# First G loaded in four pieces, its transposes moved forward, seven U blocks multiplied as split pairs, and 110 instead of 108 blocks of U ahead of the loop

## The chip, the cores and the metric

The kernel runs on one core of one Trainium2 chip. The metric is the device time of one execution in microseconds (us). The median of three runs of the kernel before the change is 1488.86 us (1487.65 to 1489.21). The engines are TensorE (PE in the profile, with its weight loads as PEld), VectorE (DVE), ScalarE (ACT), GpSimd (POOL) and SyncE (SP). ACT and SP issue ordinary DMAs, POOL issues the indirect ones that gather table rows.

## The reference

The program is one encoder layer on 512 tokens of width 1024: two kinds of attention, a LayerNorm, and then a product-key expert layer (PEER) with a gate, followed by a second LayerNorm. The change touches only the expert layer:

```
idx = e1 * 128 + e2                        # 8 heads x 16 picks = 128 experts of 16384 per token
g   = softmax(cv)                          # their weights
hpre = einsum('td,ted->te', x, U[idx])     # U: 16384 x 1024
act  = g * gelu(hpre)
out  = einsum('te,ted->td', act, V[idx])   # V: 16384 x 1024
h    = LN2(alpha*h + out + sigmoid(h @ W_g + b_g) * (p @ W_ple))
```

## The kernel before, in words

**Two ways through the experts.** The first 128 tokens (chunk 0) are served by gathers: POOL fetches one row of U, later of V, per token and expert, and DVE does the dot product or the weighted sum. The other 384 tokens are served densely. For each of the 128 blocks of 128 experts there is a matrix G (experts of the block x tokens, mostly zeros) with the router's weights. For 256 of the tokens the kernel computes gelu(U_block . h) on TensorE, multiplies it into G on DVE, and multiplies the product with the V block on TensorE, which adds up the output in PSUM. The 128 tokens in between (chunk 1, "own" in the code: `N_S = 128`) get their U values by gathers, folded into G beforehand, and only their V side is dense.

**Products before the loop.** `gate_and_leads` is a generator of TensorE work: one step is one matmul, and a block of U is eight of them (`lead_block`, line 1291) in plain float32. `LEAD` blocks of U are done so, ahead of the loop. Their gelu results (`ge`) go to a DRAM tensor for the first `SPILL = 96` blocks, and stay on chip for the others: `KEPT_K` of them in tiles that the gate no longer needs, the rest in eight `ge` tiles. U is loaded into three `raw` tiles and one `raw_u` tile by SP, in turn.

**What sets the order.** The order is written out by hand. The router (`route`), the construction of G (`build_g`, 16 steps per chunk of 128 tokens: one-hot matrices `oh_i` and `oh_j` on DVE and ACT, sixteen small products on TensorE at line 1115, results `g_st` copied out by ACT at line 1128) and the row gathers of the own chunk (`own_rows`) and of chunk 0 (`beside`) are generators too. `run_pe(amount)` puts TensorE steps worth `amount` us behind them into the queue, so the constants `WAIT`, `LAG`, `PACE`, `OWN_G` and so on decide how much U work stands between two steps of the G work. The G of a chunk begins with three transposes (line 1090) of its expert numbers and weights. Chunks 2 and 3 come first; the own chunk's G is built last, because it needs the gathered values. Finished G goes out to DRAM in quarters (`send`, line 1073, by ACT).

**The first G.** The loop reads G in groups of eight blocks (`GB = 8`), of twelve token groups each, ten of them from DRAM. The group of the first eight blocks (`first_g`) is loaded before the own chunk is built, in one DMA of eight token groups (line 1447), after all quarters have been sent.

**The loop.** It goes over 128 blocks (`order`): DVE multiplies `ge` into G (line 1598), ACT and DVE cut V and G into a high part in the reduced type float32r and a rest (`split`, line 110), and TensorE does 18 matmuls of 512 columns (line 1551). From the ninth block on (`KEPT = 8`) it also does the blocks of U that are left (`expert_in`: split pair, 24 matmuls of 256 columns at lines 129 to 131), one per iteration, until U is done. Gathers for chunk 0 are spread over the iterations in proportion to a weight (1 with a block of U, `LATE = 0.57` without). `load_g` loads the next group of G in four parts; in which iterations is set by one condition:

```
if n % GB == (GB // 2 - 1 + q if n < KEPT + 128 - LEAD + 4 else GB - 2 + q // 2):
    gt_next = load_g(n // GB * GB + GB, 3 - q if n < GB else q, gt_next, q == 0)
```

Part 0 opens a new tile. For `LEAD = 108` the bound is 32, and for 110 it is 30.

**Waits between DMAs.** Each DMA that SP or ACT issues has one of eight semaphores, in turn, and waits for the DMA that had it before. An engine that issues a DMA stands still until that one has landed.

## Time and profile before

| | |
|---|---|
| median of three runs | 1488.86 us (1487.65 to 1489.21) |
| the profiled execution | 1489.54 us, of it a span of 1487.8 us from the first instruction to the last |
| attention and first LayerNorm | 0 to about 320 us |
| router scores, routing, first G | about 320 to 712 us |
| G of chunk 3, then of the own chunk | 712 to 893 us |
| loop: with blocks of U / without | 893 to 1066 us / 1066 to 1468 us |
| second LayerNorm | 1468 to 1488 us |
| busy in the loop from 1070 to 1468 us | PE 397.62, DVE 384.54, ACT 154.82, POOL 226.59 of 398 us |

The page gives busy time by engine and groups of instructions, the table of stretches gives it for each stage, the timeline lists instructions with the idle time just before them and what ended it, and the tables of waits add up such idle times. "raw" in a row is a tile of U, V or a weight, and the line tells which. A plain float32 matmul appears as two records. The name `ACTq` or `SPq` stands for the DMA issues of that engine.

### The profile page before, as it was taken

How to read it: one execution, taken by the hardware profiler on the slowest of the kernel's cores; microseconds unless marked ns; L12 is line 12 of the kernel's file. 1: busy time of each engine (PE TensorE's matmuls, PEld its weight loads, DVE VectorE, ACT ScalarE, POOL GpSimd, SP SyncE). 2: the span in 40 equal slices, each digit the busy share in tenths (PEclk: the TensorE clock that was granted, in tenths of full speed). 3: DMA queues.
4: the chain of work that ended last, by engine and by line, in shares of the span. 5: the costliest groups of instructions: out<-in, count | busy, mean ns of one | idle time of the engine just before them, and what ended most of it. 6: DMA issues, size and time to landing. Idle time of an engine off the chain costs nothing.

```text
span 1487.8 us, 22518 instructions
## 1 busy us (share of the span) xinstructions
PE 1450.2 (97%) x7693; PEld 1212.4 (81%) x7693; DVE 1268.5 (85%) x2736; ACT 638.4 (43%) x1203; POOL 570.7 (38%) x520
## 2 busy tenths in 40 slices
PE   9999999999999999999998999999999999999997
PEld 5788777788888878888887888988888888888775
DVE  7376786579998979998776987999899999999997
ACT  3355776243221554212555763444343333333433
POOL 1013110010014544344442435665555666666630
PEclk9999999999999999999999999999999999999999
DMA  7333340175239999999999999999999999999992
GB/s 255 99 111 92 97 128 30 29 245 170 100 125 351 334 416 415 405 324 336 392 416 410 376 396 369 415 417 417 401 393 411 412 412 411 412 412 412 411 362 85
DMA packets 196851, 453.82 MB, mean 305 GB/s; under 512 B 18945, under 2 KB 96897, under 8 KB 196738
## 3 DMA queue, kind: packets, MB, share of 16 engines
q1 hardware_dynamic: 119168, 211.72, 38.6%
q0 software_dynamic: 57984, 207.12, 35.5%
q10 hardware_dynamic: 19586, 33.57, 5.9%
q8 instruction: 60, 0.98, 0.2%
q14 instruction: 53, 0.43, 0.1%
HBM read 411.70 MB, written 37.75 MB: 302 GB/s over the span
## 4 chain that ended last, share of the span: by engine, by line
PE 56%; DMA 22%; DVE 9%; issue 6%; ACT 4%; POOL 3%; SPq 0%; ACTq 0%; DVEq 0%; POOLq 0%
PE acc L1551 16%; DMA raw<-in_v_rows_dram 11%; PE mm L1291 6%; PE hp L1291 5%; DMA ge_dram<-ge 4%; PE mm L129 4%; PE mm L131 4%; PE mm L130 4%; PE pj L129 3%; PE pj L130 3%; PE pj L131 3%; DMA v_raw<-in_v_rows_dram 3%; PE hp L129 1%; PE hp L131 1%; PE hp L130 1%
## 5 line engine op out<-in xcount | busy, mean ns | idle before, releaser
L110 DVE TENSOR_TENSOR wlo<-raw,whi 128x1024 fp32r<-128x1024 f32 (+4 forms) x113 | 131.5, 1164 | 45.7 <-ACT whi L110 45.4
L110 ACT CAST a_hi<-gt 128x384 fp32r<-128x384 f32 (+2 forms) x128 | 64.9, 509 | 242.4 <-DVE gt L1598 179.5
L110 ACT CAST whi<-raw 128x1024 fp32r<-128x1024 f32 (+4 forms) x113 | 113.0, 1001 | 106.9 <-PE mm L130 47.3
L1291 PE MATMUL mm<-whole,raw 128*128 128x256 f32 x672 | 153.1, 381 | 1.5 <-DMA raw<-in_uT_dram 1.5
L1174 POOL DMA_INDIRECT whi<-in_u_rows_dram,s_ix x51 | 64.2, 1259 | 218.5 <-DVE cand L994 129.7
L1551 PE MATMUL acc<-hTh,a_hi 128*128 128x512 f32 x456 | 141.8, 391 | 0.1
L1551 PE MATMUL acc<-hTl,a_hi 128*128 128x512 f32 x456 | 141.2, 390 | 0.0
L1551 PE MATMUL acc<-hTh,a_lo 128*128 128x512 f32 x456 | 140.9, 389 | 0.0
L1291 PEld LDWEIGHTS mm<-whole,raw 128*128 128x128 f32 x672 | 125.6, 190 | 17.9 <-DMA raw<-in_uT_dram 1.9
L1534 POOL DMA_INDIRECT gat<-in_v_rows_dram,i_sel x64 | 100.8, 1574 | 55.0 <-DVE base L1536 39.5
L110 ACT CAST hTh<-v_raw 128x1024 fp32r<-128x1024 f32 x74 | 77.8, 1051 | 55.9 <-PE acc L1551 23.1
L1551 PEld LDWEIGHTS acc<-hTl,a_hi 128*128 128x128 f32 x456 | 85.4, 188 | 18.3 <-DVE hTl L110 0.4
L1551 PEld LDWEIGHTS acc<-hTh,a_lo 128*128 128x128 f32 x456 | 85.4, 188 | 18.2 <-DVE a_lo L110 0.3
L1551 PEld LDWEIGHTS acc<-hTh,a_hi 128*128 128x128 f32 x456 | 84.1, 188 | 17.2 <-ACT a_hi L110 1.1
L110 DVE TENSOR_TENSOR hTl<-v_raw,hTh 128x1024 fp32r<-128x1024 f32 x74 | 90.2, 1219 | 6.4 <-ACT hTh L110 6.4
L1551 PE MATMUL acc<-wlo,a_hi 128*128 128x512 f32 x300 | 92.8, 390 | 0.2
L1551 PE MATMUL acc<-whi,a_hi 128*128 128x512 f32 x300 | 92.8, 391 | 0.1
L1551 PE MATMUL acc<-whi,a_lo 128*128 128x512 f32 x300 | 92.6, 390 | 0.0
L1174 POOL DMA_INDIRECT wlo<-in_u_rows_dram,s_ix x51 | 61.9, 1213 | 68.3 <-DVE s_dot L1176 56.0
L1519 POOL DMA_INDIRECT gat<-in_u_rows_dram,i_sel x52 | 69.1, 1329 | 45.2 <-DVE hdot L1525 34.1
L1536 DVE SCALAR_TENSOR_TENSOR base<-gat,hdot,base 128x1024 f32<-128x1024 f32 x64 | 82.0, 1281 | 1.0
L1273 ACT ACTIVATE ge<-mm 128x256 f32<-128x256 f32 x78 | 29.6, 380 | 110.4 <-PE mm L1291 100.5
(415 smaller groups left out, 3815.7 us busy)
## 6 DMA issues: line engine op xcount, KB each, us to landing
raw<-in_uT_dram SPq DMA_DIRECT2D x80, 512.0 KB, 7.8
v_raw<-in_v_rows_dram SPq DMA_DIRECT2D x78, 512.0 KB, 13.2
raw<-in_v_rows_dram SPq DMA_DIRECT2D x48, 512.0 KB, 13.8
g_dram<-g_st ACTq DMA_DIRECT2D x40, 512.0 KB, 12.1
ge_dram<-ge ACTq DMA_DIRECT2D x96, 128.0 KB, 7.0
ge<-ge_dram SPq DMA_DIRECT2D x96, 128.0 KB, 13.0
gt<-g_dram SPq DMA_DIRECT2D x30, 384.0 KB, 13.9
raw_u<-in_uT_dram SPq DMA_DIRECT2D x19, 512.0 KB, 7.8
```

The source lines that it names most:

```text
L110: cut = nc.scalar.copy(hi, src), nc.vector.tensor_tensor(lo, src, r32(hi), op=OP.subtract)
L129: nc.tensor.matmul(ps, a[0], b[0], start=start, stop=False)
L130: nc.tensor.matmul(ps, a[0], b[1], start=False, stop=False)
L131: nc.tensor.matmul(ps, a[1], b[0], start=False, stop=stop)
L1174: nc.gpsimd.indirect_dma_start(out=u[:], out_offset=None, in_=u_rows, in_offset=bass.IndirectOffsetOnAxis(ap=ix[:, k:k + 1], axis=0))
L1273: nc.scalar.activation(ge, ps[:, :N_U], AF.Gelu)
L1291: nc.tensor.matmul(ps[:, :N_U], raw[:, k], whole[:, k, :], start=(k == 0), stop=(k == 7))
L1519: nc.gpsimd.indirect_dma_start(out=u[:], out_offset=None, in_=u_rows, in_offset=bass.IndirectOffsetOnAxis(ap=i_sel[:, c, k:k + 1], axis=0))
L1534: nc.gpsimd.indirect_dma_start(out=u[:], out_offset=None, in_=v_rows, in_offset=bass.IndirectOffsetOnAxis(ap=i_sel[:, c, k:k + 1], axis=0))
L1536: nc.vector.scalar_tensor_tensor(base[c], u, hdot[:, c, k:k + 1], base[c], op0=OP.mult, op1=OP.add)
L1551: nc.tensor.matmul(acc[c][hf], a[:, cs], b[:, hf * 512:(hf + 1) * 512], start=(n == 0 and i == 0), stop=(n == 127 and i == 2))
```

## The change

It has six parts. (1) `LEAD` goes from 108 to 110, so the loop has 18 blocks of U instead of 20; `KEPT_K` goes from 4 to 6 to hold two more results on chip. (2) While the own chunk's G is built, every second block of U is cut into a split pair (`cut_next`: cast on ACT, rest on DVE) while the block before it is multiplied. `lead_block` multiplies such a block as 24 float32r matmuls, with the eight that use the rest of h at the end. The pairs lie in the half of `hTh` and `hTl` that also takes the first two cut V blocks. (3) The first G is loaded in four DMAs of two token groups each, in steps 6 to 9 of the own chunk's build (`load_first`), and the quarters that are left are sent one per step instead of all at once before it. (4) `LAG` goes from 6.0 to 1.0 and `WAIT` from 8.4 to 3.0, so less U work stands ahead of the transposes of the own chunk and of chunk 3. Four rows of `beside` (`GAP_ROWS`) come between those transposes and the first step, instead of one, and `MORE_G` adds 0.1 us of U work to each step. (5) The G tensor in DRAM is split into the part of the own chunk (`g_own`) and the rest. (6) Through `LEAD`, the bound in `load_g`'s condition moves from 32 to 30.

```diff
--- before.py
+++ after.py
@@ -34,23 +34,28 @@
 GT = 32
 G_PARTS = 4
 GB = 8
-LEAD = 108
+LEAD = 110
 SPILL = 96
 KEPT = 8
-KEPT_K = 4
+KEPT_K = 6
 FIRST = 40
 PACE = 1.1
 AHEAD = 14.0
-LAG = 6.0
+LAG = 1.0
 BESIDE = 26
 PRE = BESIDE
 OWN = 1.2
 OWN_G = 0.7
 OWN_G_LATE = 4.0
 SEAM = 7.0
-WAIT = 8.4
+WAIT = 3.0
+FIRST_G_AT = 6
+FIRST_PARTS = 4
+GAP_ROWS = 4
 OWN_LATE = 10.0
 LATE = 0.57
+MORE_G = 0.1
+CUT_EVERY = 2
 OT = 8
 W_SCALE = 32768.0
 G_SPLIT = 1.0
@@ -831,7 +836,8 @@
     NTG = N_D // GT
     u_rows, v_rows = A["u_rows"], A["v_rows"]
     ge_dram = dram.tile([SPILL, 128, N_U], F32, name="ge_dram")
-    g_dram = dram.tile([NTG, 128, 128 * GT], F32, name="g_dram")
+    g_own = dram.tile([N_S // GT - 2, 128, 128 * GT], F32, name="g_own")
+    g_dram = dram.tile([NTG - N_S // GT, 128, 128 * GT], F32, name="g_dram")
 
     pB = ctx.enter_context(tc.tile_pool(name="pB", bufs=1, reuse_waits="tile"))
     base = [pB.tile([128, D], F32, name=f"base_{c}") if c < NGC else h[c] for c in range(4)]
@@ -1070,8 +1076,18 @@
         if parts:
             g, t, x = parts.pop(0)
             n = 128 // G_PARTS
-            nc.scalar.dma_start(g_dram[g][:, x * n * GT:(x + 1) * n * GT],
+            to = g_own[g] if g < N_S // GT else g_dram[g - N_S // GT]
+            nc.scalar.dma_start(to[:, x * n * GT:(x + 1) * n * GT],
                                 t[:, x * n:(x + 1) * n].rearrange("p i t -> p (i t)"))
+
+    def load_first(x):
+
+        while parts and parts[0][0] >= N_S // GT:
+            send()
+        n = (NTG - N_S // GT) // FIRST_PARTS
+        g = slice(x * n, (x + 1) * n)
+        nc.sync.dma_start(first_g[:, N_S // GT + g.start:N_S // GT + g.stop].rearrange("p g i t -> p g (i t)"),
+                          g_dram[g, :, SPILL * GT:(SPILL + GB) * GT].rearrange("g p x -> p g x"))
 
     def run_pe(amount):
         nonlocal due
@@ -1147,6 +1163,8 @@
             for i in range(2 * OI_ACT):
                 nc.scalar.activation(oh[:, i // 2, :, i % 2], iota, AF.Abs, bias=ne[:, OT * q + i:OT * q + i + 1])
             nc.scalar.activation(oh[:, 0:OI_ACT], oh[:, 0:OI_ACT], AF.Relu, bias=1.0, scale=-1.0)
+            if c == NGC and 0 <= q - FIRST_G_AT < FIRST_PARTS:
+                load_first(q - FIRST_G_AT)
             if ahead:
                 sums = products(*ahead)
                 due -= G_SPLIT
@@ -1196,10 +1214,11 @@
     v_cut = {}
 
     v_homes = [[flat_of(t, 2 * x, 2) for t in (hTh, hTl)] for x in range(2)]
+    cutting, n_cut, in_parts = False, 0, {}
 
     def beside():
 
-        nonlocal due
+        nonlocal due, cutting
         raw = []
 
         def cut(n):
@@ -1209,6 +1228,8 @@
         for k, x in enumerate(rows(i_sel[:, 0, :], h[0], hdot[:, 0, :], range(BESIDE))):
             if k == BESIDE - 12:
                 due -= SEAM
+            if k == BESIDE - 7:
+                cutting = False
             if k in (BESIDE - 12, BESIDE - 5):
                 n = len(raw)
                 raw.append(rw.tile([128, D], F32, name="h_s" if n else "gb"))
@@ -1221,6 +1242,7 @@
         yield 1.2
 
 
+    PRODUCT_C = 0.36
     PRODUCT_U, PRODUCT_G = 0.49 * N_U / 288, 0.69
     raws = []
     tasks = []
@@ -1278,6 +1300,17 @@
 
     last = []
 
+    def cut_next():
+
+        nonlocal n_cut
+        if cutting and raws and raws[0][0] % CUT_EVERY == 0 and raws[0][0] not in in_parts:
+            i, raw = raws[0]
+            hi, lo = [t.rearrange("p (k n) -> p k n", n=128) for t in v_homes[n_cut % 2]]
+            n_cut += 1
+            in_parts[i] = hi, lo
+            tasks.extend([lambda: nc.scalar.copy(hi, raw), nothing,
+                          on_vector(1.2, lambda: nc.vector.tensor_tensor(lo, raw, r32(hi), op=OP.subtract))])
+
     def lead_block():
 
 
@@ -1287,13 +1320,23 @@
         nonlocal u_done
         i, raw = raws.pop(0)
         ps = psH.tile([128, 512], F32, name="hp") if gating else ps_tile("mm", 4)
+        parts_u = in_parts.pop(i, None)
+        terms = [(a, b, k) for x in (((0, 0), (0, 1)), ((1, 0),)) for k in range(8) for a, b in x]
         for k in range(8):
-            nc.tensor.matmul(ps[:, :N_U], raw[:, k], whole[:, k, :], start=(k == 0), stop=(k == 7))
+            if k == 1:
+                cut_next()
+            if parts_u:
+                for n in range(3 * k, 3 * k + 3):
+                    a, b, at = terms[n]
+                    nc.tensor.matmul(ps[:, :N_U], parts_u[a][:, at], (hTh, hTl)[b][:, 1, at, :], start=(n == 0),
+                                     stop=(n == 23))
+            else:
+                nc.tensor.matmul(ps[:, :N_U], raw[:, k], whole[:, k, :], start=(k == 0), stop=(k == 7))
             if k == 3 and last:
                 leave_u(*last.pop())
             if k % 2 and tasks:
                 tasks.pop(0)()
-            yield PRODUCT_U
+            yield PRODUCT_C if parts_u else PRODUCT_U
         last.append((i, ps))
         u_done = i + 1
         if i in home_of:
@@ -1397,7 +1440,7 @@
     pe_work = gate_and_leads()
     own, own_due = None, 0.0
 
-    def run(steps, share=0.0, n=2):
+    def run(steps, share=0.0, n=2, more=0.0):
 
         nonlocal own_due
         for amount in steps:
@@ -1406,7 +1449,7 @@
                 for _ in range(n if own else 0):
                     run_pe(next(own, 0.0))
                 continue
-            run_pe(amount)
+            run_pe(amount + more)
             own_due += amount * share
             while own and own_due > 0:
                 x = next(own, None)
@@ -1440,18 +1483,16 @@
             pass
         own = None
         run_pe(LAG)
-
-        while parts:
-            send()
+        cutting = True
+
         first_g = pX.tile([128, NTG, GB, GT], F32, name="gt1")
-        nc.sync.dma_start(first_g[:, 128 // GT:].rearrange("p g i t -> p g (i t)"),
-                          g_dram[128 // GT:, :, SPILL * GT:(SPILL + GB) * GT].rearrange("g p x -> p g x"))
         build = build_g(NGC, *held)
         next(build)
-        run_pe(next(side))
+        for _ in range(GAP_ROWS):
+            run_pe(next(side))
         own = side
         own_due = -OWN_G_LATE
-        run(build, OWN_G)
+        run(build, OWN_G, more=MORE_G)
         for x in own:
             run_pe(x)
         while parts:
@@ -1472,7 +1513,8 @@
         if q < 2:
             nc.scalar.copy(t[:, N_S // GT - 2 + q], g_last[q][:, i:i + GB, :])
         nc.sync.dma_start(t[:, g].rearrange("p g i t -> p g (i t)"),
-                          g_dram[g, :, i * GT:(i + GB) * GT].rearrange("g p x -> p g x"))
+                          (g_dram[g.start - N_S // GT:g.stop - N_S // GT] if q else g_own)
+                          [:, :, i * GT:(i + GB) * GT].rearrange("g p x -> p g x"))
         return t
 
     def block_of_u(n):
```

**TensorE, from the end of chunk 3's G to the first products of the own chunk.** In these rows `raw` and `raw_u` are blocks of U, `whole` is h in float32, and `e1s`, `e2s` and `gws` are the own chunk's expert numbers and weights. Before:

```order
L1115 MATMUL tr<-oh_i,oh_j 128x128
L1291 MATMUL mm<-whole,raw_u 128x256 x4
L1291 MATMUL mm<-whole,raw 128x256 x13
L1090 MATMUL tr<-ident,e1s 128x128
L1090 MATMUL tr<-ident,e2s 128x128
L1090 MATMUL tr<-ident,gws 128x128
L1291 MATMUL mm<-whole,raw 128x256 x11
L1115 LDWEIGHTS oh_j
```

With the change:

```order
L1131 MATMUL tr<-oh_i,oh_j 128x128
L1334 MATMUL mm<-whole,raw 128x256 x4
L1106 MATMUL tr<-ident,e1s 128x128
L1106 MATMUL tr<-ident,e2s 128x128
L1106 MATMUL tr<-ident,gws 128x128
L1334 MATMUL mm<-whole,raw 128x256 x5
L1334 MATMUL mm<-whole,raw_u 128x256 x8
L1334 MATMUL mm<-whole,raw 128x256 x8
L1331 MATMUL mm<-hTh 128x256
L1331 MATMUL mm<-hTl,hTh 128x256
```

The transposes stand behind 4 instead of 17 float32 matmuls, and 21 of them, and nine of the first split block, instead of 11 come between the transposes and the first products. From there to the last products the queue held 95 float32 matmuls; it now holds 81 and 159 of the split blocks, and behind the last products 23 instead of 33.

**SP, around the first G.** `gt` is the tile of the first G. Before:

```order
L1251 DMA raw_u<-in_uT_dram 128x1024
L1251 DMA raw<-in_uT_dram 128x1024
L1447 DMA gt_7619<-g_dram 128x8x256
L1251 DMA raw<-in_uT_dram 128x1024 x2
L1251 DMA raw_u<-in_uT_dram 128x1024
L1251 DMA raw<-in_uT_dram 128x1024 x3
```

With the change:

```order
L1273 DMA raw<-in_uT_dram 128x1024 x3
L1089 DMA gt_7570<-g_dram 128x2x256
L1273 DMA raw_u<-in_uT_dram 128x1024
L1273 DMA raw<-in_uT_dram 128x1024
L1089 DMA gt_7570<-g_dram 128x2x256
L1273 DMA raw<-in_uT_dram 128x1024 x2
L1089 DMA gt_7570<-g_dram 128x2x256
L1236 DMA gb<-in_v_rows_dram 128x1024
L1089 DMA gt_7570<-g_dram 128x2x256
```

One load of 1 MB became four of 256 KB, the first of them six loads of U further back.

**SP, in the loop, iterations 27 to 31.** `gt1` is the tile of the group that begins with iteration 32. Before, its four parts are loaded in iterations 27 to 30. With the change:

```order
L1515 DMA gt1_10175<-g_own_3024 128x2x256
L1531 DMA raw_10178<-in_v_rows_dram 128x1024
L1515 DMA gt1_10175<-g_dram_3025 128x2x256
L1531 DMA v_raw_10215<-in_v_rows_dram 128x1024
L1515 DMA gt1_10175<-g_dram_3025 128x3x256
L1531 DMA raw_10249<-in_v_rows_dram 128x1024
L1635 DMA ge_10255<-ge_dram_3023 128x256
L1515 DMA gt1_10286<-g_own_3024 128x2x256
L1515 DMA gt1_10286<-g_dram_3025 128x2x256
L1531 DMA v_raw_10291<-in_v_rows_dram 128x1024
L1635 DMA ge_10295<-ge_dram_3023 128x256
L1515 DMA gt1_10286<-g_dram_3025 128x3x256 x2
```

Three parts are loaded under the early rule (iterations 27 to 29), and in iterations 30 and 31 the late rule opens the tile anew and loads all four: three loads, 896 KB, more than before. The second set waits for the first.

## The prediction

> **What bounds the kernel now.** I read the page first, then busy time by stage, then the waits of TensorE, then the timelines around each wait.
>
> ```profile
> span 1487.8 us, 22518 instructions
> PE 1450.2 (97%) x7693; PEld 1212.4 (81%) x7693; DVE 1268.5 (85%) x2736; ACT 638.4 (43%) x1203; POOL 570.7 (38%) x520
> ```
>
> ```profile
> 684.00:753.00 69.00, 69.00 (x392) 60.88 (x391) 55.87 (x96) 29.25 (x69) 32.95 (x27) 1.00 0.98 377
> 753.00:895.00 142.00, 133.14 (x905) 116.23 (x904) 110.20 (x178) 91.33 (x226) 48.77 (x41) 0.99 1.00 396
> 895.00:1070.00 175.00, 175.00 (x998) 154.40 (x997) 161.21 (x249) 70.57 (x102) 105.85 (x79) 1.00 1.02 408
> 1070.00:1468.00 398.00, 397.62 (x1742) 324.56 (x1741) 384.54 (x487) 154.82 (x221) 226.59 (x147) 1.00 0.99 390
> ```
>
> The columns are the stretch, its length, busy time of PE, PEld, DVE, ACT and POOL, the granted clock, DMA share and GB/s. TensorE sets the time: it is idle for 8.9 us while the own chunk's G is built (753 to 895 us), and for almost nothing behind it. In the loop DVE (384.54 of 398 us) and the DMAs are nearly full too. The waits of TensorE from 753 to 895 us are these:
>
> ```profile
> PE tr L1115 <- ACT g_st L1128: 5.1, 5, 1.7
> PE mm L1291 <- DMA raw<-in_uT_dram: 1.5, 1, 1.5
> PE tr L1115 <- DVE oh_j L1156: 1.2, 2, 0.9
> PE tr L1115 <- ACT oh_i L1149: 1.1, 1, 1.1
> ```
>
> So a change pays if it takes work off TensorE's queue, or these waits, and if in the loop the DMAs keep pace.
>
> **The price of a block of U.** Ahead of the loop blocks of 16 records (8 float32 matmuls) follow each other (TensorE's timeline), and in the loop (chain of waits) a split block stands between two groups of 18 output matmuls:
>
> ```profile
> 684.16 3.62 PE L1291 MATMUL mm<-whole,raw_u 128*128 128x256 f32 x16
> 687.61 10.52 PE L1291 MATMUL mm<-whole,raw 128*128 128x256 f32 x48
> ```
>
> ```profile
> 933.29 4.11 PE acc L1551 x18
> 940.27 4.11 PE acc L1551 x18
> ```
>
> A float32 block takes 687.61 - 684.16 = 3.45 us (0.43 per matmul). A split block takes 940.27 - 933.29 - 4.11 = 2.87 us. Ahead of the loop TensorE gets two float32 blocks more, +6.90, and seven blocks (168 matmuls in the new queue) become split pairs, 7 x (3.45 - 2.87) = -4.06. Together **+2.84 us**. The page "FP8 and Floating Point Precision" of the Trainium skill ("TensorE Precision Notes") says that true FP32 takes four passes; three passes would then cost 2.59 us by estimate, the seven blocks would save 6.0, and the term would be +0.9. The loop's 2.87 has the same 24 matmuls, so I go by the row.
>
> **Waits ahead of the loop.** Two of them have a cause that the change takes away. These are rows of the timelines of DVE, ACT, TensorE and SP, in order of time; in brackets is the idle time ahead of an instruction and what ended it.
>
> ```profile
> 810.35 0.42 DVE L1098 CAST eT<-tr 128x256 f16<-128x256 f32 x1 [8.18 <-PE tr L1090]
> ...
> 811.29 2.24 ACTq L1073 DMA_DIRECT2D g_dram<-g_st  x3
> 813.58 0.28 ACT L1101 ACTIVATE eT<-tr 128x128 f16<-128x128 f32 x1 [5.41 <-DMA ge_dram<-ge]
> ...
> 816.08 0.22 PE L1115 MATMUL tr<-oh_i,oh_j 128*128 128x128 f16 x1 [1.09 <-ACT oh_i L1149]
> 816.60 1.03 PE L1115 MATMUL tr<-oh_i,oh_j 128*128 128x128 f16 x15 [0.30 <-DVE oh_j L1156]
> ...
> 819.76 0.38 SPq L1447 DMA_DIRECT2D gt<-g_dram  x1
> ...
> 827.99 1.56 PE L1291 MATMUL mm<-whole,raw 128*128 128x256 f32 x6 [1.46 <-DMA raw<-in_uT_dram]
> ```
>
> DVE stands idle for 8.18 us because 17 float32 matmuls lie ahead of the transposes; then ACT is held for 5.41 us, ending in three sends of G in a row; TensorE waits 1.09 + 0.30 = 1.39. With the change the transposes come 13 matmuls (5.6 us) earlier, 21 x 0.43 + 9 x 0.12 = 10.1 us of work stand behind them, and the sends are spread over the steps. What DVE and ACT need from the transposes to the first products took 6.2 us (810.35 to 816.60) with ACT held up, so the 1.39 goes. The rows of `beside` ahead of the casts of the transposes' results (three more of 1.22 us on DVE, below) take 3.7 us of the 8.18 that stood idle. The 1.46 for a block of U comes from the first G, which stood at the head of SP's queue until 819.76 with the loads of U behind it. In four pieces, in steps 6 to 9, its sources have long landed, and it holds up nobody; each piece is 256 KB that needs to be there only at the loop's start, some 30 us later. **-2.85 us** for both.
>
> The rest, 6.0 us, are waits for ACT (`g_st`) and one of 0.86 for DVE, in two places: in the last steps of chunk 3, where three or four float32 matmuls stand between products, and around 860 us, where 32 products follow each other without any. Both places are in the new queue as well (3, 4, 4 and again 32). I leave them at 6.0. For the bounds: all of it could vanish (-6.0), or grow by what the casts cost ACT, seven of 1.04 us. The first rows show such a cast on ACT and its rest on DVE, a row of `beside`, sixteen products in the chain of waits, and the end of the build; then come two stretches of it with the columns as above:
>
> ```profile
> 880.35 1.04 ACT L110 CAST hTh<-gb 128x1024 fp32r<-128x1024 f32 x1
> 881.43 1.23 DVE L110 TENSOR_TENSOR hTl<-gb,hTh 128x1024 fp32r<-128x1024 f32 x1 [4.57 <-ACT hTh L110]
> ...
> 842.65 1.22 DVE L1176 CUSTOM_DVE_ANT_0 whi<-whi,h 128x1024 f32<-128x1024 f32 x1
> ...
> 723.50 0.92 PE tr L1115 x16
> ...
> 878.27 1.08 PE L1115 MATMUL tr<-oh_i,oh_j 128*128 128x128 f16 x16
> ...
> 887.14 0.41 DVE L110 TENSOR_TENSOR a_lo<-gt,a_hi 128x256 fp32r<-128x256 f32 x1
> ```
>
> ```profile
> 830.00:850.00 20.00, 20.00 (x146) 17.75 (x144) 17.31 (x27) 15.61 (x39) 7.47 (x6) 1.00 1.03 412
> 850.00:870.00 20.00, 17.17 (x133) 15.03 (x132) 18.81 (x30) 14.91 (x38) 8.62 (x7) 0.91 1.03 418
> ```
>
> Cover for them: from the first to the last products TensorE now has 81 x 0.43 + 159 x 0.12 + 16 x 0.92 = 68.6 us (0.12 is 2.87 / 24) instead of 95 x 0.43 + 14.7 = 55.6. ACT is busy for 30.5 of 40 us in the two stretches, which makes 52 of 68.6, and with 7.3 for casts 60. DVE is busy for 36.1 of 40; over the old build of 55.6 us and 5.7 of waits that is 55, less three rows of `beside`, plus seven rests of 1.23, 60 again. Both fit under 68.6, ACT with little left for its standstills at DMAs. Without that cover the casts cost their 7.3 us. Behind the last products stand 23 float32 matmuls, 9.9 us, instead of 33. ACT and DVE had the first block's `a_lo` ready (887.55) 8.4 us behind the end of the last products (878.27 + 0.92), so it just holds. The two results in `KEPT_K` tiles and the split DRAM tensor cost nothing: no instruction or byte is added, since the same `ge` rows are written by the same instructions of ACT.
>
> Ahead of the loop: +2.84 - 2.85 = 0.0.
>
> **The loop.** TensorE loses two split blocks: -2 x 2.87 = -5.74. Whether that arrives depends on the DMAs.
>
> ```profile
> 1066.00:1090.00 24.00, 18.86 (x31) 1.00 0.99 361
> 1112.00:1135.00 23.00, 22.40 (x38) 1.00 1.04 410
> 1135.00:1200.00 65.00, 63.31 (x74) 1.00 1.04 412
> 1200.00:1300.00 100.00, 99.05 (x117) 1.00 1.04 412
> ```
>
> ```profile
> SPq L1593 <- DVE gt L1598: 6.5, 3, 2.7
> ```
>
> ```profile
> 1371.41 0.61 PE L1551 MATMUL acc<-hTh,a_lo 128*128 128x512 f32 x2
> 1372.13 0.73 PE L1551 MATMUL acc<-whi,a_hi 128*128 128x512 f32 x2
> ```
>
> ```profile
> 1343.19 13.27 DMA raw<-in_v_rows_dram
> ...
> 1356.82 13.77 DMA raw<-in_v_rows_dram
> ```
>
> ```profile
> gt<-g_dram SPq DMA_DIRECT2D x18, 384.0 KB, 13.5
> ```
>
> First come stretches with DVE alone (busy, clock, DMA share, GB/s), then SP's longest wait from 1066 to 1090 us, two rows of TensorE's timeline, two of the chain of waits, and the landing time of a part of G. From 1112 us on the transfers stand at 410 to 412 GB/s, and at 1371 us the even beat of 0.45 us per pair breaks (0.72): TensorE waits for a V block, and the chain of waits runs through the loads of V there. So DMA decides the last hundred us. Out of the loop go two blocks of U (1.05 MB), and in come the three needless parts of G (0.92 MB): -0.13 MB, -0.3 us at 412 GB/s. What can still be gained is the hole at 1066 to 1090 us, where SP, far ahead, waited for DVE to free its buffers: 24 x (412 - 361) / 412 = 3.0 us. With two iterations fewer of 6.98 us, SP gets less far ahead, and the needless loads fill what is left. So **-3.3 us**. Bounds: -5.74 if the DMAs give way, -0.3 if the hole stays. DVE loses two rests (2.4 us) and its own 5.1 us of idle in that hole, and agrees.
>
> The page "DMA: Bandwidth & Descriptors" of the Trainium skill ("Bandwidth", "Measured") gives 425 GB/s for a core that streams alone, 3% above 412; by that estimate the DMAs would not be at their limit, and the loop would give most of the 5.74. The flat row speaks for 412.
>
> **Sum.** 0.0 - 3.3 = -3.3 us. The profiled execution has 1489.54 (span 1487.8 and 1.74 around it), so 1486.2; it lies 0.7 above the median of the runs, and from that it is 1488.86 - 3.3 = **1485.6 us**.
>
> **Rivals.**
> - More is won: the DMAs give way (-5.0 of -5.74), and the waits for ACT shrink by 3 because chunk 3's transposes, too, stand 14 matmuls earlier in the new queue. -8 us, 1481. For it: DVE's long idle time ahead of the transposes is gone. Against it: the places with little U work between products are unchanged.
> - The loop gives nothing back: the second set of `gt1` loads waits until the third needless part has landed (13.5 us, the median for 384 KB), SP stands still for that time and loses its lead, so the hole only moves. -0.3 us, 1488.6, no change. For it: the lead is what pays later. Against it: gathers and the loads in flight go on meanwhile.
> - Slower: the own chunk's G becomes ACT's. A cast in ACT's queue delays `g_st` and with it the next products; TensorE then waits with each step. From the point where ACT's 60 us and its standstills at DMAs (5.41 above) exceed 68.6, each cast costs its 1.04: +7, less 3 from the loop: +4, 1493. For it: `g_st` is the longest wait already. Against it: 13 us more U work per build.
>
> **How the numbers follow.** A measurement of this kernel can tell about 0.2%, 3 us, from no change. Chances: forecast 0.40 (own range 1483 to 1488), more 0.25, nothing back 0.20, slower 0.15. The forecast lies at the edge of 0.2% (1485.9), so a little over half of it counts as faster: 0.23 + 0.25 = 0.48 faster; 0.17 + 0.19 = 0.36 within; 0.01 + 0.15 = 0.16 slower. For 8 in 10 the range reaches into the first and the last case: 1480 to 1492.5.
>
> **What would show it.** Right: no wait for `raw` and none at the own chunk's first products; the loop begins within 2 us of 893; iterations with U still 6.98; the stretch of 361 GB/s gone; TensorE's waits late in the loop up by some 2 us. Wrong: `g_st` waits well above 5.1 us (slower), or a loop shorter by 5 us and more (more is won), or a new hole of the DMAs around iteration 30 (nothing back).

## The result: slower by 0.5%

The changed kernel takes 1496.97 us (median of 6 runs, 1496.05 to 1499.67) against 1488.86 (6 runs, 1487.65 to 1492.3) for the kernel before, measured beside it: a ratio of 1.0051, 95% interval 1.0039 to 1.0064. In a second comparison it was 1498.11 against 1489.39, ratio 1.0061 (1.0046 to 1.0076). So it is some 8 us slower, not 3 faster, and outside the range. Medians and ratios, here and below, leave out four executions in which the same program took far longer (1822.56 to 6546.08 us).

The page of the changed kernel, its first lines; then three stretches with the columns as in the prediction (length, busy PE, PEld, DVE, ACT, POOL, clock, DMA share, GB/s):

```profile
span 1496.0 us, 22614 instructions
PE 1453.5 (97%) x7733; PEld 1216.2 (81%) x7733; DVE 1275.1 (85%) x2741; ACT 642.8 (43%) x1210; POOL 576.1 (39%) x520
```

```profile
753.00:895.00 142.00, 131.76 (x954) 117.96 (x953) 110.76 (x170) 92.42 (x217) 49.11 (x39) 0.98 1.01 392
895.00:1070.00 175.00, 170.41 (x946) 149.59 (x945) 154.96 (x243) 69.07 (x106) 99.31 (x73) 0.98 0.98 389
1070.00:1468.00 398.00, 397.15 (x1742) 324.69 (x1741) 386.99 (x495) 151.59 (x219) 237.28 (x153) 1.00 1.01 398
```

From 753 to 895 us TensorE is idle for 10.2 us (8.9 before) at a clock of 0.98 (0.99 before), and from 895 to 1070, where it was never idle before, for 4.6 us, at a clock of 0.98 (1.00 before). The loop's first output matmul starts at 899.96 us instead of 893.29, and from there to the end of the last one it takes 585.97 us instead of 584.27. So 6.7 us are lost ahead of the loop and 1.7 in it, where 3.3 were to be won.

**Ahead of the loop.** TensorE's waits from 753 to 895 us have new owners:

```profile
PE tr L1131 <- DVE oh_j L1174: 5.3, 5, 2.1
PE mm L1331 <- ACT hTh L1311: 2.8, 1, 2.8
PE tr L1131 <- ACT g_st L1144: 1.4, 2, 0.9
PE tr L1131 <- DVE s_dot L1194: 0.7, 1, 0.7
```

The wait for a block of U (1.5) and the one at the own chunk's first products (1.39) are gone, as forecast, and the waits for `g_st` fell from 5.1 to 1.4. In their place stand 5.3 us for `oh_j` and 2.8 for a cast. The timelines of SP, ACT, DVE and TensorE around the largest show how that comes about (in brackets the idle time ahead of the instruction and what ended it); between them stands a row of the chain of waits:

```profile
835.59 0.99 SPq L1089 DMA_DIRECT2D gt<-g_dram  x1
```

```profile
836.69 14.83 DMA raw_u<-in_uT_dram
```

```profile
844.07 1.09 ACT L1144 ACTIVATE g_st<-tr 128x512 f32<-128x512 f32 x2
851.54 1.04 ACT L1311 CAST hTh<-raw_u 128x1024 fp32r<-128x1024 f32 x1 [6.38 <-DMA raw_u<-in_uT_dram]
852.62 1.23 DVE L1312 TENSOR_TENSOR hTl<-raw_u,hTh 128x1024 fp32r<-128x1024 f32 x1 [6.28 <-ACT hTh L1311]
852.64 0.58 PE L1331 MATMUL mm<-hTh 128*128 128x256 f32 x1 [2.85 <-ACT hTh L1311]
859.86 0.23 PE L1131 MATMUL tr<-oh_i,oh_j 128*128 128x128 f16 x1 [1.58 <-DVE oh_j L1174]
```

The load of a U block is issued behind a piece of the first G and needs 14.83 us. Its cast stands in ACT's queue a block ahead and stops ACT for 6.38 us, DVE stands still for 6.28 behind it, and then DVE's `oh_j` is late step after step.

That is one execution. In a second profiled one of the same kernel TensorE's waits from 684 us to the loop come to 10.3 us, nearly the same, but with other owners; the cast of the same block waits there for 3.33 us, and TensorE not at all for the cast:

```profile
PE tr L1131 <- ACT g_st L1144: 7.0, 7, 2.1
PE tr L1131 <- DVE oh_j L1174: 3.3, 4, 1.5
```

```profile
850.72 1.04 ACT L1311 CAST hTh<-raw_u 128x1024 fp32r<-128x1024 f32 x1 [3.33 <-DMA raw_u<-in_uT_dram]
```

So the sum is alike in the two executions, while the engine that comes last at a step is not.

**In the loop** the loss is at one place. Rows of SP's, ACT's, DVE's and TensorE's timelines, with one of the chain of waits in a fence of its own:

```profile
1033.73 0.44 SPq L1515 DMA_DIRECT2D gt<-g_dram  x1
1038.64 0.43 SPq L1515 DMA_DIRECT2D gt<-g_dram  x1
...
1055.03 0.71 ACT L1514 COPY gt<-g_st 128x256 f32<-128x256 f32 x2 [12.17 <-DMA gt<-g_dram]
1056.18 0.56 DVE L115 TENSOR_TENSOR a_lo<-gt,a_hi 128x384 fp32r<-128x384 f32 x1 [11.39 <-ACT a_hi L115]
1056.20 1.22 PE L1593 MATMUL acc<-hTh,a_hi 128*128 128x512 f32 x2 [4.59 <-ACT a_hi L115]
```

```profile
1038.64 16.29 DMA gt<-g_dram
```

With the bound at 30, three parts of a group of G are loaded in iterations 27 to 29, and in iteration 30 the tile is opened again and all four parts come anew. Ahead of the first two parts ACT copies token groups of the own chunk into the tile (line 1514). That copy must wait until the needless loads into the same place have landed, 16.29 us after the last was issued. It stands in ACT's queue ahead of the casts `a_hi`, so DVE and TensorE stand too. TensorE waits there for 4.6 us, and behind the wait its granted clock is low (TensorE alone: length, busy, clock, DMA share, GB/s):

```profile
1056.00:1066.00 10.00, 9.79 (x46) 0.77 0.97 328
```

That is 10 x 0.23 = 2.3 us more. The two blocks of the loop that are hit (the 25th and 26th) take 20.8 us instead of 14.0 before.

### The profile page after: what moved, and what is told of

It is laid out like the page before. It is cut to its first block, busy times and chain, and to the rows that moved or that the text cites. A ratio compares the mean times of both kernels' runs of the same rounds, so it can differ in the third digit from the quotient of the medians.

```text
span 1496.0 us, 22614 instructions
## 1 busy us (share of the span) xinstructions
PE 1453.5 (97%) x7733; PEld 1216.2 (81%) x7733; DVE 1275.1 (85%) x2741; ACT 642.8 (43%) x1210; POOL 576.1 (39%) x520
## 4 chain that ended last, share of the span: by engine, by line
PE 41%; DMA 21%; DVE 19%; issue 11%; ACT 4%; POOL 4%; SPq 0%; ACTq 0%; DVEq 0%; POOLq 0%
PE acc L1593 8%; DMA v_raw<-in_v_rows_dram 5%; PE mm L1334 4%; PE mm L134 4%; DMA gt<-g_dram 3%; PE mm L135 3%; PE mm L136 3%; PE hp L1334 3%; PE pj L134 3%; PE pj L135 3%; PE pj L136 3%; DMA raw<-in_v_rows_dram 3%; DVE base L1578 2%; DMA ge<-ge_dram 2%; DMA ge_dram<-ge 2%
## 5 line engine op out<-in xcount | busy, mean ns | idle before, releaser
L1334 PE MATMUL mm<-whole,raw 128*128 128x256 f32 x640 | 147.9, 383 | 0.0
L1334 PEld LDWEIGHTS mm<-whole,raw 128*128 128x128 f32 x640 | 119.5, 191 | 15.0
L115 DVE TENSOR_TENSOR a_lo<-gt,a_hi 128x384 fp32r<-128x384 f32 (+2 forms) x128 | 69.6, 545 | 22.0 <-ACT a_hi L115 22.0
```

The source lines that it names most:

```text
L115: cut = nc.scalar.copy(hi, src), nc.vector.tensor_tensor(lo, src, r32(hi), op=OP.subtract)
L1334: nc.tensor.matmul(ps[:, :N_U], raw[:, k], whole[:, k, :], start=(k == 0), stop=(k == 7))
```

## The experiments

Waits are TensorE's from 684 us to the loop's first output matmul. The loop is from that matmul to the end of the last one; both are of the profiled execution of each kernel. Medians and ratios are against the kernel before, run beside it (medians 1488.61 to 1489.44). The code excerpts show the lines that change; `...` stands for others that belong to the edit.

| kernel | median us | ratio, 95% interval | loop begins | loop us | waits us |
|---|---|---|---|---|---|
| before | 1488.86 | | 893.29 | 584.27 | 8.9 |
| changed | 1496.97 | 1.0051 (1.0039 to 1.0064) | 899.96 | 585.97 | 10.2 |
| changed, again | 1498.11 | 1.0061 (1.0046 to 1.0076) | 900.29 | 585.80 | 10.3 |
| changed, bound 32 | 1494.35 | 1.0035 (1.0022 to 1.0049) | 900.17 | 579.47 | 10.8 |
| the same again | 1494.99 | 1.0035 (1.0021 to 1.0049) | 902.79 | 579.98 | 12.4 |
| changed, no split pairs | 1506.14 | 1.0104 (1.0085 to 1.0123) | 911.62 | 585.76 | 14.5 |
| bound 32, no split pairs | 1496.36 | 1.0046 (1.0031 to 1.0062) | 906.38 | 579.71 | 10.6 |
| changed, 108 blocks | 1488.71 | 1.0009 (0.9994 to 1.0025) | 894.95 | 584.17 | 12.1 |
| before, 110 blocks, bound 32 | 1492.60 | 1.0024 (1.0015 to 1.0034) | 901.83 | 579.83 | 9.7 |
| before, 110 blocks, bound 30 | 1497.60 | 1.0048 (1.0034 to 1.0062) | 903.37 | 585.36 | 9.6 |
| bound 32, first G as before | 1504.31 | 1.0101 (1.0083 to 1.0119) | 913.72 | 579.74 | 19.9 |
| bound 32, old order | 1493.38 | 1.0029 (1.0015 to 1.0044) | 899.10 | 581.23 | 9.2 |
| bound 32, both as before | 1493.23 | 1.0025 (1.0015 to 1.0035) | 893.95 | 583.68 | 8.1 |
| bound 32, half rows | 1489.61 | 1.0003 (0.9989 to 1.0016) | 894.60 | 580.32 | 8.5 |
| before, 110, half rows | 1488.03 | 0.9991 (0.9977 to 1.0005) | 895.90 | 579.68 | 6.9 |
| bound 32, no casts | 1499.82 | 1.0068 (1.0053 to 1.0083) | 909.12 | 579.84 | 16.9 |
| bound 32, casts of one column | 1498.97 | 1.0057 (1.0041 to 1.0074) | 909.04 | 579.81 | 17.1 |
| bound 32, multiply late | 1493.66 | 1.0032 (1.0019 to 1.0044) | 901.75 | 580.01 | 12.9 |
| no casts, multiply late | 1488.45 | 0.9999 (0.9990 to 1.0008) | 901.36 | 581.52 | 12.4 |
| before, 106 blocks | 1486.07 | 0.9976 (0.9965 to 0.9987) | 886.27 | 587.40 | 9.4 |

The same program ahead of the loop begins its loop up to 5 us apart (911.62 and 906.38 without split pairs), so a single profile does not decide a few us there; the medians do. The length of the loop does not scatter so: with 110 blocks it is 579.5 to 580.3 us in ten of the thirteen executions with bound 32, longer in three, and 585.4 to 586.0 in all four with bound 30. For "no casts, multiply late" the profiled execution is the slowest of its twelve (1495.2 us, the others 1486.4 to 1491.5), so its row of the trace says little. The profiled executions of "changed, bound 32" (1491.58 us) and "bound 32, both as before" (1489.63) are the fastest of theirs, that of "changed, no split pairs" (1509.67) the slowest.

### The needless loads

```diff
-                    if n % GB == (GB // 2 - 1 + q if n < KEPT + 128 - LEAD + 4 else GB - 2 + q // 2):
+                    if n % GB == (GB // 2 - 1 + q if n < 32 else GB - 2 + q // 2):
```

Bound 32 in the changed kernel:

> The changed kernel with one number in it altered: the bound in the condition of `load_g` is 32 again (as with 108 blocks ahead of the loop) instead of 30, so no part of G is loaded twice. Theory A (the needless loads hold ACT: its copy into the re-opened `gt1` tile waits 12.17 us for them, DVE then 11.39, TensorE 4.59 and 2 more): both breaks at 1055 to 1065 us go, the loop falls from 584.4 us by 6 to 7 to about 578, the whole from 1497.0 to about 1490. Rival B (only the bytes count: the duplicate parts cost 0.92 MB of DMA time at 412 GB/s): -2.2 us, 1494.8, and the wait of ACT's copy moves to another place. Rival C (the loop is held by the last hundred us of DMA-bound V loads, and what is won at 1055 is given back there): no change, 1497.

The loop is 6.5 us shorter, and with it the waits at 1055 us are gone (895 to 1070 us, columns as above):

```profile
895.00:1070.00 175.00, 175.00 (x976) 153.72 (x975) 162.57 (x254) 71.73 (x107) 104.02 (x77) 1.00 0.99 398
```

By the median it gains 2.6 us, near rival B's 2.2, by the trace 6.5. So both kernels ran once more side by side:

> The changed kernel itself once more, beside the same with bound 32, since the traces say 5.8 us for the needless loads (loops of 585.0 and 579.2 us) and the medians of different hours 2.6. If the trace is right: 5 to 6 us apart, about 1499 against 1494; if the medians are: 1497 against 1494.4.

> The changed kernel with bound 32 once more, beside the changed kernel: 1494.4 as before, 5 to 6 us below the changed kernel by the traces, 2.6 by the earlier medians.

3.1 us apart in the medians, 5.8 in the loops. And the kernel before with 110 blocks alone, with the two bounds:

> The kernel before the change with one part of it alone: 110 blocks of U ahead of the loop (and six kept results), with the bound in `load_g` at 32, so that no part of G is loaded twice. Theory A (two float32 blocks cost 6.90 us of TensorE ahead of the loop, and the loop gives back what it gave with bound 32, 582.8 - 578.6 = 4.2): the loop begins at 900.2 and takes 578.6; 1488.9 + 2.7 = 1491.6. Rival B (ahead of the loop the DMAs, at 412 to 418 GB/s from 750 us on, are full, and two U blocks more also lengthen the waits): the loop begins at 903 or later and the time is 1494 or more. Rival C (the loop gives back the whole 5.74): 1490.0.

> The kernel before with 110 blocks of U ahead of the loop and the bound at 30, as in the change, so that parts of G are loaded twice; nothing else. Against the same with bound 32 (1492.6, a loop of 579.4 us): theory A (ACT's copies into the re-opened tile wait for the needless loads) says 5.8 to 6.8 us slower in the loop around 1055 us and 1498 to 1499; rival B (only the bytes) 1494.8; if the 2.6 us by which the medians of the changed kernel differ are the whole effect, 1495.2.

5.0 us apart in the medians, 5.5 in the loops. By the traces theory A holds in each pair: the break stands in all four executions with bound 30 and in none with 32, and the bytes alone (2.2 us) don't explain 5.5 to 6.5 us of loop. How much of it the median shows is not settled better than 2.6 to 5.0 us here, and 9.8 in the pair without split pairs; why less than the trace's 6 us arrives in the first pairs stays open.

### The blocks ahead of the loop

110 blocks alone (bound 32) cost +3.4 us against the 1489.23 beside it: theory A. The loop gives back 584.27 - 579.83 = 4.4 us of the 5.74 that TensorE no longer does there, against 6.90 ahead of it. It first gives back all of it: from the loop's first output matmul to that of its 81st block it is 378.8 us instead of 384.6. In the last 48 blocks 1.4 us are lost again. The other way round (the bound stays 32, since `KEPT` falls with it):

```diff
-LEAD = 108
+LEAD = 106
-KEPT_K = 4
+KEPT_K = 2
-KEPT = 8
+KEPT = 6
```

> The kernel before with two blocks of U fewer ahead of the loop, 106 instead of 108, with two kept results instead of four and the loop's U work from its seventh block on instead of the ninth. If what was measured for 110 holds in the other direction (6.9 us of TensorE less ahead of the loop, 3.6 us more in it), it is 3.3 us faster than the kernel before, 1485.9. If the loop takes the whole 5.74 of TensorE work, as it has no slack on that side, 1.2 us faster, 1488. If the results come too close to their use (a block's result two steps earlier needed than now), the loop waits and it is slower, 1491.

The loop begins 7.0 us earlier and is 3.1 us longer; 1486.07 against 1489.49 is 3.4 us faster, and it beats both kernels. The sign of this part of the change was wrong for this kernel.

### Everything else in the change

> The changed kernel with 108 blocks of U ahead of the loop and four kept results again (the bound is then 32 by itself), and the other parts as changed. Theory A (the extra blocks cost what they do ahead of the loop, 6.90 us, and the other parts together bring nothing, since 6.67 - 6.90 = -0.2): the loop begins at about 893, it takes the 582.8 us that it took before, and the time is 1488.6, no change against the kernel before. Rival B (the two blocks more stretch the queue and make the waits at 852 to 865 us): those 4 us go too, and the time is about 1485. Rival C (in the loop the old hole in the transfers is back but the rest of the change has moved loads too): slower than before by 1 to 3 us, 1490 to 1492.

```diff
-LEAD = 110
+LEAD = 108
-KEPT_K = 6
+KEPT_K = 4
```

No difference that can be measured, 1.0009 (0.9994 to 1.0025). The split pairs, the order and the pieces together bring nothing, where the prediction had -4.06 - 2.85 = -6.9 us. Taken out one by one (each with 110 blocks):

> The changed kernel without the split pairs ahead of the loop: all 110 blocks stay plain float32 (no casts on ACT, no rests on DVE there); everything else stays. Theory A (the cast, standing in ACT's queue before its U block has landed, holds ACT for 6.4 us at 851 us, and DVE and TensorE behind it): the waits of TensorE between 753 and 900 us fall from 10.2 by about 4 to 6, its work there grows by 7 x 0.39 = 2.7, so the loop begins about 1.3 us earlier and the time is about 1495.7. Rival B (the pieces of the first G in SP's queue make the load of U late, and the cast only shows it): the block of U is as late as before, TensorE itself now waits for it, the 2.7 us of work come on top, and the time is about 1499.7. The break in the loop at 1055 us stays in both.

> The changed kernel with both edits: bound 32, and no split pairs ahead of the loop. If the two causes are independent, the two gains add up: 1497.0 - 6.8 - 1.3 = about 1489, no different from the kernel before the change. If the loop only passes on a part of what is won ahead of it (DMA-bound at its end), the gain over the bound alone is zero and the time is about 1490 to 1491. If the casts were worth it, this is 2.7 us slower than with the bound alone, 1493.

```diff
-        cutting = True
+        cutting = False
```

Without split pairs it is slower, by 2 us with bound 32 (near the third case, 2.7) and by 9 with bound 30. There neither theory had it so: the waits do not fall, they change owner. ACT and DVE have no cast to wait for, and DVE then waits for something else. Of the kernel with bound 30 (with bound 32 the same wait is 3.69 us):

```profile
870.10 0.43 DVE L1640 TENSOR_TENSOR gt<-gt,g_raw 128x256 f32<-128x256 f32 x1 [7.40 <-DMA gt<-g_dram]
```

That row is taken up below. Now the first G and the order (with bound 32, set as above):

> The changed kernel with bound 32 and with the first G loaded as before: all quarters sent and one DMA of 1 MB ahead of the own chunk's build, instead of four pieces in its steps 6 to 9. Theory P (the pieces, in SP's queue between the loads of U and in the ring of eight semaphores that SP and ACT share, hold both up: a U block issued right behind a piece was 6.38 us late for its cast, a send of ACT waited 3.25 us for a piece): the waits of TensorE from 840 to 866 us, 3.5 to 6 us, shrink to 1 or 2, the loop begins at 897 instead of 900.2, and the time is about 1491 against 1494.4. Rival Q (the waits come from full DMAs, whatever the order in the queue): they move to where the one big load and the sends now stand (around 815 us), SP's standstill of 11.5 us is back with a wait of 1.5 for a block of U, and the time stays at 1494 to 1496.

```diff
+        while parts:
+            send()
         first_g = pX.tile([128, NTG, GB, GT], F32, name="gt1")
+        nc.sync.dma_start(first_g[:, N_S // GT:].rearrange("p g i t -> p g (i t)"),
+                          g_dram[:, :, SPILL * GT:(SPILL + GB) * GT].rearrange("g p x -> p g x"))
...
-FIRST_G_AT = 6
+FIRST_G_AT = 99
```

10 us slower, not 3 faster: theory P was wrong. SP's longest waits ahead of that one load (line 1491 in this kernel), and what TensorE then waits for:

```profile
SPq L1491 <- DMA g_dram<-g_st: 10.0, 1, 10.0
SPq L1491 <- DMA ge_dram<-ge: 7.3, 1, 7.3
```

```profile
PE mm L1334 <- DMA raw<-in_uT_dram: 12.5, 1, 12.5
```

SP stands still for 17.3 us with the loads of U behind it. With the transposes early, less U work lies ahead of this place, and TensorE's wait for a block of U is 12.5 us instead of 1.5. The pieces are needed once the order is changed.

> The changed kernel with bound 32 and with the order around the transposes as before (LAG 6.0, WAIT 8.4, one row of chunk 0 between the own chunk's transposes and its first step, no extra U work per step); casts and pieces stay. Theory G (with less U work ahead of the transposes, chunk 3's build loses its head start, and the waits for DVE's `oh_j` of 2.11 us at 780 and for ACT at 816, not there before, come from it): they go, and 2 to 3 us with them, 1491.5. Rival H (the early transposes did what they were meant to do): the 1.39 us of waits at the own chunk's first products come back, and the time is 1495.8.

> The changed kernel with bound 32, the order around the transposes as before and the first G as before: of the change only 110 blocks and the split pairs are left. Against the kernel before with 110 blocks alone (sent together with this one) it shows what the casts do by themselves. Theory A (casts are hidden, seven blocks save 7 x 0.39 to 7 x 0.58): 2.7 to 4.1 us faster than that kernel, about 1488. Rival B (a cast that stands in ACT's queue ahead of its U block delays ACT and then TensorE wherever the first G stands): what is saved is lost in waits of TensorE behind `hTh` and `oh_j`, and it is no faster than that kernel, 1491 to 1492.

```diff
-LAG = 1.0
+LAG = 6.0
-WAIT = 3.0
+WAIT = 8.4
-GAP_ROWS = 4
+GAP_ROWS = 1
-MORE_G = 0.1
+MORE_G = 0.0
```

(the second with the edits of the first G as well). 1493.38 and 1493.23: the two cannot be told from each other, nor from 110 blocks alone (1492.60). In the last kernel the casts saved TensorE work and its loop begins at 893.95, but it is 583.68 us long. TensorE's timeline from the end of the build's last products to the loop's start:

```profile
888.48 2.37 PE L1334 MATMUL mm<-whole,raw_u 128*128 128x256 f32 x10
890.69 3.62 PE L1334 MATMUL mm<-whole,raw 128*128 128x256 f32 x16
...
894.78 0.50 PE L1597 MATMUL acc<-hTh,a_hi 128*128 128x512 f32 x1 [0.24 <-ACT ge L1295]
897.17 1.19 PE L1597 MATMUL acc<-hTh,a_lo 128*128 128x512 f32 x4 [0.51 <-DVE a_lo L115]
...
916.86 0.73 PE L1597 MATMUL acc<-hTh,a_hi 128*128 128x512 f32 x2 [0.81 <-ACT a_hi L115]
```

Only 13 float32 matmuls of U (26 records, 5.5 us) are left behind the last products, and the loop waits 1.6 us in these rows for what ACT and DVE have yet to cut: the U work ran out too soon. That explains a part of the 3.9 us by which this loop is longer than that of 110 blocks alone; the rest stays open.

### Are full DMAs the reason?

> The changed kernel with bound 32, in which the row gathers ahead of the loop (`own_rows` and `beside`) fetch only the first 64 of their 128 rows, and DVE multiplies only these 64 partitions (in the same time); the dot products of the other half are left out. It takes 256 KB from each of 154 gathers, 40 MB in all, and nothing from TensorE, DVE or ACT. Theory D (from 710 to 870 us the DMAs are full, 412 to 418 GB/s, and what TensorE saves there only runs into loads of U that are late): the waits of TensorE from 753 to 900 us fall from 10.8 to 4 or less, with a full clock, and the time falls from 1494.4 by 8 to 10 to about 1485. Rival E (the waits come from the order of the work on ACT and DVE): they stay, and the time falls by 2 or less.

> The kernel before with 110 blocks and bound 32, with the same halved row gathers. Theory D: it gains too, but keeps its TensorE work of seven blocks more at full price (7 x 0.39 to 7 x 0.58 = 2.7 to 4.1 us) and the waits of 1.39 us behind the late transposes: it is then 4 to 5 us slower than the changed kernel with halved gathers, about 1489 to 1490, while with full gathers it was 1.8 us faster. Rival E: the two stand to each other as with full gathers, this one 1.8 us faster.

```diff
-            nc.gpsimd.indirect_dma_start(out=u[:], out_offset=None, in_=u_rows,
-                                         in_offset=bass.IndirectOffsetOnAxis(ap=ix[:, k:k + 1], axis=0))
+            nc.gpsimd.indirect_dma_start(out=u[:64], out_offset=None, in_=u_rows,
+                                         in_offset=bass.IndirectOffsetOnAxis(ap=ix[:64, k:k + 1], axis=0))
...
```

(DVE's product behind it is cut to the same 64 rows.) Both gain the same, 4.7 and 4.6 us against their full versions, and they stand to each other as before (1.6 us apart, the changed one slower). That is rival E's order, though neither theory has the size (8 to 10, or 2 and less). But fewer bytes did not make the DMAs idle. A stretch of the changed kernel with half rows, TensorE alone (busy, clock, DMA share, GB/s):

```profile
750.00:770.00 20.00, 18.33 (x124) 1.00 1.04 349
```

The share stays at 1.02 to 1.04 from 710 to 810 us while the rate falls to 286 to 351 GB/s. So the bytes of the gathers are not why the change brings nothing; whether DMAs with time to spare would alter that, no run shows. In the changed kernel with half rows two of DVE's waits remain that the kernel before does not have:

```profile
DVE hTl L1314 <- ACT hTh L1313: 9.5, 5, 2.6
DVE gt L1642 <- DMA gt<-g_dram: 4.5, 1, 4.5
```

### The casts, and the wait that takes their place

> The changed kernel with bound 32, in which the seven casts and rests of U blocks are left out. TensorE still does the split products of these blocks, on what stands in the tiles (so these seven blocks' results are not those of U), with one float32 matmul on the loaded block in place of the first three, so that it still waits for the load. ACT and DVE have nothing to do with U there. Theory S (ACT's standstill at a cast whose block is late is what costs) and theory W (the work of casts and rests, 7 x 1.04 and 7 x 1.23 us, is what costs) both say that the waits of TensorE from 753 to 900 us fall from 10.8 to 5 to 7 and the time from 1494.4 to 1489 to 1491. Rival N (the casts were hidden; the waits come from the rest of the new order): 1493 to 1495.

> The same with casts and rests of a single column: ACT still stands in its queue until the U block has landed, but then has next to nothing to do, and DVE neither (the blocks' results are wrong in all other columns). Theory S: no better than with full casts, 1493 to 1494.4. Theory W: as good as without casts, 1489 to 1491. Both at once: halfway, 1492. Rival N: no difference between the three.

```diff
-            tasks.extend([lambda: nc.scalar.copy(hi, raw), nothing,
-                          on_vector(1.2, lambda: nc.vector.tensor_tensor(lo, raw, r32(hi), op=OP.subtract))])
+            tasks.extend([nothing, nothing, on_vector(1.2, nothing)])
```

(the second: the same two instructions on one column.) In the first, TensorE also does one float32 matmul on the loaded block in place of the first three. Both are 4 to 5.5 us slower than with full casts. All theories failed, and the two don't tell standstill from work. DVE's and TensorE's rows in the kernel without casts, then the same multiply in the changed kernel and, as the last row, in the kernel before:

```profile
869.79 0.43 DVE L1641 TENSOR_TENSOR gt<-gt,g_raw 128x256 f32<-128x256 f32 x1 [9.63 <-DMA gt<-g_dram]
870.87 0.29 PE L1131 MATMUL tr<-oh_i,oh_j 128*128 128x128 f16 x1 [6.34 <-DVE oh_j L1174]
```

```profile
862.34 0.42 DVE L1640 TENSOR_TENSOR gt<-gt,g_raw 128x256 f32<-128x256 f32 x1
```

```profile
847.14 0.42 DVE L1598 TENSOR_TENSOR gt<-gt,g_raw 128x256 f32<-128x256 f32 x1
```

It is the loop's first instruction on DVE (it multiplies `ge` into the first G). In DVE's queue it does not stand behind the build, but in its middle, between two `oh_j`. Before the change the first G was issued at 819.76 and there in time. In the changed kernel the four pieces go out until 851.18:

```profile
842.90 0.43 SPq L1089 DMA_DIRECT2D gt<-g_dram  x1
...
850.20 0.43 SPq L1089 DMA_DIRECT2D gt<-g_dram  x1
...
851.18 0.43 SPq L1089 DMA_DIRECT2D gt<-g_dram  x1
```

The multiply needs all of them. In the kernel without casts they go out until 854.77, and DVE stands at the multiply until 869.79. With its casts the changed kernel is already late there, and the wait is hidden; without them it shows, 9.63 us long. To test it, this one instruction was moved behind the build, 34 rows later in DVE's queue, and nothing else:

```diff
-            nc.vector.tensor_tensor(dn, dn, ge.rearrange("p (g t) -> p g t", t=GT), op=OP.mult)
+            first = nc.vector.tensor_tensor(dn, dn, ge.rearrange("p (g t) -> p g t", t=GT), op=OP.mult)
+            if n == 0:
+                tc.keep_in_program_order(first)
```

> The changed kernel with bound 32, and with one instruction of DVE moved: the loop's first multiply of `ge` into the first G (0.42 us) stands behind the own chunk's build in DVE's queue, instead of in it (34 rows later). Theory M (the pieces of the first G, issued until 853 to 856 us and 10 to 15 us on their way, are needed by this multiply at about 860 us, in the middle of the build, and DVE stands still for them wherever it isn't late for another reason): the execution can't be held there any more; its waits behind `oh_j` from 855 to 870 us shrink, and the median falls from 1494.7 (two sets of runs: 1494.35 and 1494.99) by 1 to 3, to about 1492.5. Rival C (the casts' late U blocks come first, and the multiply only shows where they are gone): no change, 1494 to 1495.

> The kernel without casts and rests of U ahead of the loop (its seven blocks' results are not those of U), with the same one instruction of DVE moved behind the build. Theory M: DVE's 9.63 us at 869 us and TensorE's 6.34 and 1.46 behind it go, with the half clock that follows; the time falls from 1499.8 by 6 to 8 to 1492 to 1494. If it then lies below the kernel with casts and the multiply moved, the casts cost more than nothing; if it lies at the same time, they are hidden. Rival (something else held DVE there): 1498 to 1500.

Without casts it brings 11.4 us (1499.82 to 1488.45), more than the 6 to 8 expected: theory M is shown. With casts it brings 1 us (1494.99 and 1494.35 to 1493.66), within the intervals no difference. And between the last two kernels of this pair, 1493.66 and 1488.45, lies what the casts cost when nothing else stands in their place: **5.2 us**. Whether that is ACT's and DVE's work or ACT's standstill at late blocks is open; the casts of one column were run with the multiply still in the build, where DVE stands at it for 6.87 us. Nor was the kernel without split pairs run with the multiply moved, so whether the pairs pay there is open too (they save 3.2 us of TensorE, below, by estimate).

## Why the prediction was wrong

By ratios, the loss is 0.24% for 110 blocks, about 0.11% more for the rest of the change (0.09% with 108 blocks; neither can be told from nothing), and 0.16 to 0.26% for the needless loads: 0.51 to 0.61%. By the traces 6.7 us were lost ahead of the loop, where the forecast was 0.0, and 1.7 in it, where the forecast was -3.3.

- **Blocks ahead of the loop, +6.90, and the loop, -3.3: near in their sum, by luck.** 110 blocks alone cost 3.4 us, where the terms say 3.6. But that kernel has bound 32 and no needless loads, which the -3.3 counts as 2.2 us of bytes. Without them the same reckoning says 1.05 MB at 412 GB/s, 2.5 us, and the hole, 3.0: 5.5 us, of which 4.4 came. With them, in the changed kernel, the loop is 1.7 us longer. The stretch at 361 GB/s closes, as forecast, but it does not need the needless loads for that: from 1066 to 1090 us there are 406 GB/s with bound 30 and 413 with bound 32. The page "DMA: Bandwidth & Descriptors" of the Trainium skill ("Bandwidth", "Measured") would have let the loop give most of 5.74. The 4.4 lie between that and 3.3, and the rate from 1135 to 1300 us stays at 412 to 413 in the changed kernel too, so no run here shows the page's rate.

- **"The needless loads fill what is left": the step that failed in the loop.** They were costed as bytes on the DMAs, -0.13 MB net. The second rival had the right wait (the second set of loads into the tile waits for the third needless part, 13.5 us; here 16.29), but gave it to SP. The first writer into the reopened tile is ACT's copy, and behind it in ACT's queue stand the casts that TensorE needs: 5.5 to 6.5 us of loop, waits and half clock together. The sign of a wrong forecast that the prediction named was there, a new hole of the DMAs (358 GB/s from 1045 to 1056 us and 328 to 1066, where 410 and 416 stood before).

- **"Both fit under 68.6": the step that failed ahead of the loop.** The claim was that casts and rests are hidden since ACT and DVE have 60 us of work each under 68.6 of TensorE's. They cost 5.2 us, of the 7.3 named as their price without cover. A sum over the build says nothing of when an input comes: one cast whose block was late stopped ACT for 6.38 us and DVE for 6.28 in one piece (3.33 us for ACT in the other execution), while the 8.6 us of room are spread over all steps of the build. How much of the 5.2 that is, and how much the casts' own work, stays open. The slower rival (0.15) was this mechanism, a cast in ACT's queue that delays the next products. Its sign, `g_st` well above 5.1 us, is there in one execution (7.0) and not in the other (1.4), where `oh_j` comes last.

- **"-4.06": a size.** TensorE's timeline, a float32 block, a split block and its products in between, then the next float32 block:

```profile
838.82 3.67 PE L1334 MATMUL mm<-whole,raw 128*128 128x256 f32 x16
842.14 0.47 PE L1331 MATMUL mm<-hTh 128*128 128x256 f32 x1
...
843.40 1.09 PE L1131 MATMUL tr<-oh_i,oh_j 128*128 128x128 f16 x16
844.30 0.36 PE L1331 MATMUL mm<-hTl,hTh 128*128 128x256 f32 x1
...
846.17 3.62 PE L1334 MATMUL mm<-whole,raw 128*128 128x256 f32 x16
```

  846.17 - 838.82 less 0.90 for the products is 6.45 us for the pair against 6.90 for two float32 blocks: 0.45 saved each, 3.2 in all. The first split matmul behind a float32 one takes 0.31 instead of 0.12. The page "FP8 and Floating Point Precision" of the Trainium skill ("TensorE Precision Notes") would give 6.0 for the seven, by the prediction's estimate; the trace is further from it than the 2.87 of the loop was.

- **"-2.85" and "I leave them at 6.0": right for the waits it named, wrong for those that were to stay.** Both waits went, but the others grew from 6.0 to 10.2 us, so TensorE's idle time rose by 1.3 instead of falling by 2.85. The sentence on the pieces is right in one half: the pieces do keep SP from standing still (putting the one load back costs 10 us). But "each piece needs to be there only at the loop's start, some 30 us later" is false: the loop's first multiply needs all four in the middle of the build. It decides only where the casts don't (11.4 us without them, about 1 with them).

- **"The 23 float32 matmuls just hold": right for the changed kernel,** whose loop starts without a wait. With the old order, the old first G and casts 13 were left, and the loop waited.

- **The sum ahead of the loop** by the traces: +6.90 for two blocks, -3.2 for the pairs, +1.3 for waits (8.9 to 10.2 us), +1.7 for the clock (below) make 6.7, and 6.67 was measured. The agreement is better than the terms are exact: 0.59 us of the 6.67 stand already at 684 us, and it is the sum of one execution of each kernel.

## What to carry to other kernels

When a constant is changed, look for the conditions that move along with it, as the bound of `load_g` did here. Where such a condition opens a buffer anew, look for the first instruction that writes into it, and for what stands behind that instruction in its engine's queue. Work moved to an engine that has room on average still has to arrive in order: price it by what it stops if its input is late, and read from the queue's order where the consumer of a moved load really stands. And when a change has several parts, try each of them alone and with its sign turned: here the blocks moved ahead of the loop paid in the other direction (106 of them, 3.4 us faster than the kernel before).
